# A layer with three attention branches: c_q and the gates projected as columns over 512 tokens, heads transposed in 32 bits and split after the transpose

## The chip, the cores and the metric

The kernel runs on one core of a Trainium2 chip. The metric is the device time of one execution in microseconds (us), and lower is better. The core has a matrix engine (TensorE, PE in the profile; its weight loads are PEld), a vector engine (VectorE, DVE), a scalar engine (ScalarE, ACT), GpSimd (POOL), and SyncE (SP), which issues every DMA of this kernel. Each engine works through its own queue of instructions in a fixed order and waits on semaphores.

## The reference, cut to what matters

```python
h = layer_norm(x)                                   # 2048 tokens x 1024
proj = h @ w_in                                     # 1024 x 7592
(a_q, a_k, a_v, a_gate, i_q, i_k, i_w, b_q, b_k, b_v, b_gate, c_q, c_gate, m_gate) = split(proj)
# A: an indexer (i_q, i_k, i_w) picks 256 keys per query; 8 heads of a_q attend to them
o_a = dsa_attention(rope(a_q), rope(a_k), a_v, rope(i_q), rope(i_k), i_w)
o_b = diff_attention(rope(b_q), rope(b_k), b_v, lam)      # 4 heads, two softmaxes each, causal
o_c = memory_attention(c_q, mk, mv)                       # 4 heads over 256 memory tokens
y_r = (o_r * silu(r_gate)) @ w_proj_r                     # r = a, b, c
merged = sum over r of sigmoid(m_gate[r]) * y_r
out = layer_norm(2**0.25 * h + merged @ w_out)
```

All is float32. A matrix product of two float32 numbers is made of three products (`mm3`): each operand is split into a high part that the matrix engine keeps and the rest (`split`: a copy, then a subtraction).

## The kernel before

The 2048 tokens are 16 blocks of 128 (`b`), or 8 pairs of 256 (`p`). One program does it all, in this order of writing: normalise blocks 0 to 7 and transpose them (`prologue`), project a_q and the indexer columns for them (`dense_ai(0)`), find the top 256 keys of blocks 2 to 7 (`topk_group`), project b_k, b_v, b_q (`dense_b(0)`), the same for blocks 8 to 15 with two more top-k groups, then attention B (4 heads `hd`, in heads 0 and 2 from block 0 up, in 1 and 3 from block 15 down), attention A, the projections of c_q and of all gates for the upper half of the tokens (`dense_g(1)`) and the lower half (`dense_g(0)`), then branch C with the products of B and C with their output weights, then those of A (`stage1`), `w_out` and the last layer norm (`stage2`).

The order on each engine isn't the order of writing. The program is scheduled when it is built: the builder's own model of the engines decides what stands where, takes what was written first when it is ready, and moves later work up into places where an engine would stand idle. The result is one fixed queue per engine. So the matmuls of `dense_g`, which are written after both attentions but need little, are filler: they stand between the matmuls of the top-k stage and of attention B.

`dense` projects 256 columns of `w_in` per call (a job). The normalised tokens lie transposed and split in `hP[p]`, 256 tokens each. For c_q, the C gate and the merge gates the weights are the stationary side, 128 columns, and 256 tokens stream past (columns as output rows). For the A and B gates (`sg`, `idx[0]` 0 and 1) a block of 128 tokens is stationary and 256 weight columns stream past. Either way a matmul has a stationary 128x128 tile and streams 256 columns, and a pair of tokens takes 2 x 8 x 3 = 48 of them. `emit` evicts each result (tile `do`) and stores it.

`heads_out` takes the projected and rotated heads `o` of a pair from SBUF to a transposed, split form in DRAM: for each of the two blocks it splits them on DVE (tile `dt`, lines 68 and 69), transposes high and low parts together (4 matmuls against `idr`, line 223), and ACT copies the PSUM tile to `de` (line 225). It is called 64 times.

`gated` multiplies a branch's output by its stored gate (line 830, on POOL for B, on DVE for A), transposes the product on PE (line 833), and splits it on ACT and DVE (lines 835 and 836) into `oT`, which feeds the output product `yps`.

In attention B a block's chain is: logits `lg` (lines 623, 624, PE), copy with a running minimum (633, 637, DVE), exponentials (691, ACT), sums and the difference of the two softmaxes (694 to 697, DVE), transposes `pt` (703, PE), the split `pr` (66 on ACT, 69 on DVE), products `ops` (709, PE), and the norm of the output (712 to 724, ACT, DVE, POOL). `lg` has two buffers, `pt` two, `ops` one, `P` four.

## Time and profile before

| what | value |
|---|---|
| device time, median of 3 runs (range) | 2966.72 us (2961.39 to 2970.45) |
| span of the profiled execution, first to last instruction | 2965.9 us |
| PE busy | 2830.5 us (95%) |
| PEld busy | 2715.7 us (92%) |
| DVE busy | 2279.2 us (77%) |
| ACT busy | 1442.6 us (49%) |
| POOL busy | 983.2 us (33%) |
| 16 DMA engines | 40.2% of their time in the hardware queue |

The profiled execution's span is 0.8 us below the median of the runs, so times of the trace and times of runs can be used side by side. Matmuls overlap in the array: one 256-column matmul is recorded as 284 ns long, but the next one starts much sooner. The cost of a matmul in a full queue is therefore read from how many start in a stretch and not from the length of a record. "Busy" on PE counts a stretch as busy while any matmul is in the array.

### The profile page before, as it was taken

How to read it: one execution, taken by the hardware profiler on the slowest of the kernel's cores; microseconds unless marked ns; L12 is line 12 of the kernel's file. 1: busy time of each engine (PE TensorE's matmuls, PEld its weight loads, DVE VectorE, ACT ScalarE, POOL GpSimd, SP SyncE). 2: the span in 40 equal slices, each digit the busy share in tenths (PEclk: the TensorE clock that was granted, in tenths of full speed). 3: DMA queues.
4: the chain of work that ended last, by engine and by line, in shares of the span. 5: the costliest groups of instructions: out<-in, count | busy, mean ns of one | idle time of the engine just before them, and what ended most of it. 6: DMA issues, size and time to landing. Idle time of an engine off the chain costs nothing. (4 is left out here: it accounts for less than half of the span.)

```text
span 2965.9 us, 57460 instructions
## 1 busy us (share of the span) xinstructions
PE 2830.5 (95%) x21616; PEld 2715.7 (92%) x21616; DVE 2279.2 (77%) x5309; ACT 1442.6 (49%) x2806; POOL 983.2 (33%) x1064
## 2 busy tenths in 40 slices
PE   7979998999999998999999999999999999988998
PEld 6979998999999998999999999988999999978887
DVE  6499988999899998676667766658787777776655
ACT  4345673677266772333344334446566556544100
POOL 6663547242522236323324222302222222200221
PEclk9999999999999999999999999999999999999999
DMA  6554434433232234624234242273433333256532
GB/s 208 171 191 138 159 113 156 133 119 114 94 101 76 82 93 147 201 73 140 89 118 142 77 128 80 75 242 110 133 114 119 102 113 102 86 172 224 172 131 79
DMA packets 320949, 379.47 MB, mean 128 GB/s; under 512 B 26400, under 2 KB 236832, under 8 KB 320160
## 3 DMA queue, kind: packets, MB, share of 16 engines
q1 hardware_dynamic: 320672, 375.80, 40.2%
q8 instruction: 171, 2.80, 0.4%
q14 instruction: 106, 0.87, 0.1%
HBM read 236.02 MB, written 139.69 MB: 127 GB/s over the span
## 5 line engine op out<-in xcount | busy, mean ns | idle before, releaser
L72 PE MATMUL dps<-hP,w 128*128 128x256 f32 x2048 | 582.6, 284 | 15.1 <-DVE do L69 9.9
L74 PE MATMUL dps<-hP,w 128*128 128x256 f32 x2048 | 581.7, 284 | 0.0
L73 PE MATMUL dps<-hP,w 128*128 128x256 f32 x2048 | 581.2, 284 | 0.0
L72 PE MATMUL dps<-w,hP 128*128 128x256 f32 (+1 forms) x1664 | 491.1, 296 | 12.5 <-POOL w L64 3.1
L73 PE MATMUL dps<-w,hP 128*128 128x256 f32 (+1 forms) x1664 | 490.0, 295 | 0.0
L74 PE MATMUL dps<-w,hP 128*128 128x256 f32 (+1 forms) x1664 | 487.9, 294 | 0.0
L72 PEld LDWEIGHTS dps<-hP,w 128*128 128x128 f32 x2048 | 392.6, 192 | 21.6 <-DVE do L69 10.7
L74 PEld LDWEIGHTS dps<-hP,w 128*128 128x128 f32 x2048 | 392.5, 192 | 4.4 <-POOL w L69 0.3
L73 PEld LDWEIGHTS dps<-hP,w 128*128 128x128 f32 x2048 | 392.7, 192 | 3.6
L533 ACT ACTIVATE ja<-sall,thr 128x1280 bf16<-128x1280 f32 (+4 forms) x224 | 302.2, 1349 | 122.6 <-DVE thr L529 107.1
L64 POOL TENSOR_SCALAR w<-wr 128x1024 fp32r<-128x1024 f32 x120 | 135.5, 1129 | 629.5 <-PE dps L74 404.9
L72 PEld LDWEIGHTS dps<-w,hP 128*128 128x128 f32 x1664 | 324.0, 195 | 16.8 <-issue 4.3
L69 POOL TENSOR_TENSOR w<-wr,w 128x1024 fp32r<-128x1024 f32 (+1 forms) x128 | 332.1, 2595 | 15.0 <-ACT w L66 6.9
L520 DVE TENSOR_SCALAR_CACHE_REDUCE jd<-sall,thr 128x1408 bf16<-128x1408 f32 (+6 forms) x231 | 330.9, 1433 | 5.9
L73 PEld LDWEIGHTS dps<-w,hP 128*128 128x128 f32 x1664 | 324.3, 195 | 1.8
L74 PEld LDWEIGHTS dps<-w,hP 128*128 128x128 f32 x1664 | 323.8, 195 | 2.2
L691 ACT ACTIVATE P<-P,nm 128x128 f32<-128x128 f32 (+15 forms) x128 | 154.1, 1204 | 197.8 <-DVE nm L690 187.5
L626 DVE CUSTOM_DVE_ANT_0 AP<-lg,bias 128x512 f32<-128x512 f32 (+3 forms) x304 | 181.9, 619 | 68.4 <-PE lg L624 25.1
L66 ACT CAST apr<-apt 128x512 fp32r<-128x512 f32 (+1 forms) x288 | 158.4, 563 | 141.7 <-PE apt L777 108.4
L633 DVE TENSOR_SCALAR_CACHE_REDUCE P<-lg 128x512 f32<-128x512 f32 (+3 forms) x288 | 170.4, 596 | 72.3 <-PE lg L624 71.2
L493 DVE SCALAR_TENSOR_TENSOR sall<-ir,iw,sall 128x512 f32<-128x512 f32 (+3 forms) x266 | 217.1, 865 | 8.9 <-ACT ir L489 8.0
L782 PE MATMUL aops<-apr,VA 128*128 128x256 f32 x1088 | 206.7, 297 | 16.8 <-DVE apr L69 6.7
(249 smaller groups left out, 7109.2 us busy)
## 6 DMA issues: line engine op xcount, KB each, us to landing
wr<-in_w_in_dram SPq DMA_DIRECT2D x112, 512.0 KB, 3.9
tm_d<-do SPq DMA_DIRECT2D x96, 256.0 KB, 2.1
bq<-qb_d SPq DMA_DIRECT2D x128, 128.0 KB, 3.1
aq<-qa_d SPq DMA_DIRECT2D x128, 128.0 KB, 3.1
yt<-tm_d SPq DMA_DIRECT2D x64, 256.0 KB, 3.6
sg_d<-do SPq DMA_DIRECT2D x48, 256.0 KB, 2.1
ys<-sg_d SPq DMA_DIRECT2D x48, 256.0 KB, 3.1
facc<-mg_d SPq DMA_DIRECT2D x48, 256.0 KB, 4.1
```

What stands on the lines that cost most here:

```text
L66: A.copy(H, src)
L69: el.tensor_tensor(L, src, H.bitcast(F32), op=ALU.subtract)
L72: PE.matmul(ps, lH, rH, start=start, stop=False)
L73: PE.matmul(ps, lH, rL, start=False, stop=False)
L74: PE.matmul(ps, lL, rH, start=False, stop=stop)
L493: V.scalar_tensor_tensor(s[:, c0:c0 + cn], r[:, :cn], iw[:, h:h + 1], s[:, c0:c0 + cn], op0=ALU.mult, op1=ALU.add)
L520: V.tensor_scalar(jd[:, :L], sc[b], t.bitcast(F32)[:, i:i + 1], None, op0=op, op1=ALU.add, accum_out=dst[:, i:i + 1])
L533: A.activation(ja[:, :L], sc[b], AF.Sign, bias=thr.bitcast(F32)[:, i:i + 1], scale=-1.0, accum_out=cnt[:, i:i + 1])
L626: V.tensor_tensor_reduce(P[:, c0:c0 + cn], ps[:, :cn], bias[:, c0:c0 + cn], scale=-0.125, scalar=-LOW, op0=ALU.add, op1=ALU.min, accum_out ...
L633: V.tensor_scalar(P[:, c0:c0 + n0], ps[:, :n0], -0.125, None, op0=ALU.mult, op1=ALU.min, accum_out=mx[:, col, nch:nch + 1])
L691: A.activation(p[:, :L], p[:, :L], AF.Exp, bias=nm[:, c:c + 1], scale=-1.0, accum_out=sm[:, c:c + 1])
L782: PE.matmul(o_ps.rearrange("p a d -> p (a d)"), VA[:, k0 + i], pr[:, a, i].rearrange("p e q -> p (e q)"), start=(k0 + i == 0 and a == 0), ...
```

## The change

It has three parts.

1. The transposed tokens lie in one tile `H4` with two halves of 512 tokens (a quad `q` is 4 blocks). `dense` projects c_q, all the sigmoid and silu gates (also those of A and B) with the weights stationary and 512 tokens streaming: 24 matmuls of 512 columns for 128 weight columns and a quad. `emit_gate` evicts one 128x512 tile. The stored gates and c_q are laid out per quad, and the loads take 128 or 256 of 512 tokens of each row.
2. `heads_out` no longer splits on DVE first. It transposes the heads as float32 against `idf` (4 matmuls for two blocks, with 128 columns each or fewer), into one PSUM bank, and then splits on ACT and DVE into `de` on the way out. High and low parts are stored as separate planes. The loads of `qi` become four DMAs per tile in place of one; `kg` is loaded as two planes.
3. `gated` transposes the branch's output before the gate. DVE multiplies the transposed result by the transposed gate, ACT makes the high part, POOL subtracts to make the low part. The product ahead of the transposes is gone.

```diff
-    def heads_out(o, nh, d, dup, stores, p):
-        e = dp.tile([128, nh, 2, 128], F32R, name="de")
-        for i in range(2):
-            t = dp.tile([128, nh, 2 * dup, d], F32R, name="dt" if nh > 1 else "dt1", bufs=3 if nh > 1 else 2)
...
-            split(t[:, :, 0:dup], t[:, :, dup:2 * dup], src, V, V)
...
-            for c in range(nh):
-                PE.transpose(pt[:, c], t[:, c].rearrange("p a d -> p (a d)"), idr)
-            with tc.high_priority():
-                A.copy(e[:, :, i], pt)
+    def heads_out(o, groups, stores):
+        n = len(groups)
+        e = dp.tile([128, 2, n, 2, 128], F32R, name="de", bufs=4)
+        turn[0] ^= 1
+        if turn[0]:
+            pt = dq2.tile([128, n, 2, 128], F32, name="psT")
+        else:
+            pt = dqs.tile([128, n, 2, 128], F32, name="dpt", bufs=1)
+        for u, (c0, cn) in enumerate(groups):
+            for i in range(2):
+                PE.transpose(pt[:cn, u, i], o[:, i, c0:c0 + cn], idf)
+        for u0, u1 in ((0, 2),) if groups[-1][1] == 128 else ((0, n - 1), (n - 1, n)):
+            cn = groups[u0][1]
+            with tc.high_priority():
+                split(e[:cn, 0, u0:u1], e[:cn, 1, u0:u1], pt[:cn, u0:u1], A, V)
...
+        if kind in ("cq", "sg", "tm"):
+            for q in range(2 * half, 2 * half + 2):
+                for g in range(2):
+                    c = slice(g * 128, (g + 1) * 128)
+                    ps = dqs.tile([128, 512], F32, name="dps")
+                    for k in range(KT):
+                        mm3(ps, w[:, 0, k, c], w[:, 1, k, c], H4[:, q % 2, 0, k], H4[:, q % 2, 1, k], k == 0, k == KT - 1)
+                    with tc.high_priority():
+                        emit_gate(kind, idx, g, q, ps)
+            return
...
-                SP.dma_start(qi.bitcast(F32), qi_d[j][b // 2][:, :, (b % 2) * 128:(b % 2 + 1) * 128])
+                src = qi_d[j][b // 2][:, :, (b % 2) * 128:(b % 2 + 1) * 128].rearrange("a (h d) t -> a d h t", h=4)
+                for r in range(4):
+                    SP.dma_start(qi.bitcast(F32)[32 * r:32 * r + 32], src[r // 2])
...
-        SP.dma_start(s, sg_d[r][b // 2][b % 2])
-        eng.tensor_tensor(o, o, s, op=ALU.mult)
+        SP.dma_start(s, sg_d[r][b // 4][:, :, 128 * (b % 4):128 * (b % 4) + 128])
...
-            A.activation(oT[:, 0, :, t], ps, AF.Copy, scale=0.5)
-            V.scalar_tensor_tensor(oT[:, 1, :, t], ps, 0.5, oT[:, 0, :, t].bitcast(F32), op0=ALU.mult, op1=ALU.subtract)
+            V.scalar_tensor_tensor(s, ps, 0.5, s, op0=ALU.mult, op1=ALU.mult)
+            A.copy(oT[:, 0, :, t], s)
+            G.tensor_tensor(oT[:, 1, :, t], s, oT[:, 0, :, t].bitcast(F32), op=ALU.subtract)
```

The changed program is scheduled anew, so whole queues stand in another order. Two places show it.

The first is PE at the end of attention B, head 3, around the logits of block 5 (`lg` 256 columns wide). `dps` are the filler matmuls of `dense_g`, `hP_25602` is a pair of blocks, `ops`, `pt` and `lg` belong to attention B. Before:

```order
L72 MATMUL dps<-hP_25602,w 128x256
L709 MATMUL ops<-vg,pr 128x256
L73 MATMUL dps<-hP_25602,w 128x256
L74 MATMUL dps<-hP_25602,w 128x256
L72 MATMUL dps<-hP_25602,w 128x256
L623 MATMUL lg<-kg,bq 128x256
L624 MATMUL lg<-kg,bq 128x256
L73 MATMUL dps<-hP_25602,w 128x256
```

After, the same place (`lg` is now on lines 628 and 629, `pt` on 708, `ops` on 714):

```order
L714 MATMUL ops<-vg,pr 128x256 x5
L628 MATMUL lg<-kg,bq 128x256
L629 MATMUL lg<-kg,bq 128x256
L708 MATMUL pt<-idf,P 128x128 x6
L628 MATMUL lg<-kg,bq 128x256
L629 MATMUL lg<-kg,bq 128x256
L714 MATMUL ops<-vg,pr 128x256
```

No filler stands there any more: the last `dps` row of the changed program is in block 11 of head 2, and the 20 blocks of attention B behind it stand alone on PE. Before, `dps` rows go on to the end of attention B and a little past it.

The second is DVE beside the indexer's scores (`sall`), where `heads_out` of the early projections stands. Before:

```order
L493 SCALAR_TENSOR_TENSOR sall<-ir,iw,sall 128x256
L493 SCALAR_TENSOR_TENSOR sall<-ir,iw,sall 128x512
L69 TENSOR_TENSOR dt<-do,dt 128x4x64 x2
L68 CAST dt<-do 128x4x64
L493 SCALAR_TENSOR_TENSOR sall<-ir,iw,sall 128x256
```

After:

```order
L498 SCALAR_TENSOR_TENSOR sall<-ir,iw,sall 128x512
L498 SCALAR_TENSOR_TENSOR sall<-ir,iw,sall 128x128
L70 TENSOR_TENSOR de<-psT,de 128x512
L496 TENSOR_SCALAR sall<-ir,iw 128x512
L500 MEMSET sall 64x64
```

The casts and subtractions ahead of the transposes (`dt`) are replaced by one subtraction behind them (`de`), of twice the width, for a pair.

## Rows read from the trace of the kernel before

**Rows 1.** Windows by stage: us, busy us (instructions) of each engine, PE clock, DMA.
```profile
0.00:200.00 200.00, 166.43 (x1231) 162.14 (x1231) 136.28 (x248) 83.13 (x162) 131.97 (x174) 0.96 0.59 197
200.00:915.00 715.00, 675.67 (x5454) 666.54 (x5453) 662.27 (x1233) 428.37 (x822) 313.95 (x312) 0.98 0.38 123
915.00:1194.00 279.00, 263.75 (x2163) 262.06 (x2162) 249.49 (x304) 160.47 (x191) 108.45 (x48) 0.98 0.35 109
1194.00:1940.00 746.00, 741.30 (x5783) 718.60 (x5783) 510.69 (x1731) 294.84 (x563) 232.16 (x336) 1.00 0.35 109
1940.00:1956.00 16.00, 16.00 (x135) 16.00 (x134) 1.20 (x6) 1.69 (x3) 1.16 (x4) 1.00 0.80 240
1956.00:2740.00 784.00, 749.17 (x5741) 705.92 (x5740) 590.61 (x1603) 453.48 (x1033) 145.74 (x144) 0.99 0.45 136
2740.00:2966.00 226.00, 218.20 (x1120) 184.41 (x1120) 128.69 (x188) 20.66 (x35) 49.76 (x47) 0.98 0.38 132
```

**Rows 2.** Instructions on the tiles `ips`, `pf`, `lg`: ns min/median/max, first and last start.
```profile
L484 PE MATMUL ips<-KI,qi x560: 218/281/415, 136.9 to 915.2; 128*128 128x256 f32 x172, 128*128 128x128 f32 x15
...
L571 DVE TENSOR_SCALAR pf<-ja x14: 253/510/2673, 459.7 to 1181.2; 128x384 bf16<-128x384 bf16 x1, 128x512 bf16<-128x512 bf16 x1, 128x640 bf16<-128x640 bf16 x1, 128x768 bf16<-128x768 bf16 x1
...
L623 PE MATMUL lg<-kg,bq x320: 220/390/500, 1193.8 to 1922.8; 128*128 128x512 f32 x136, 128*128 128x128 f32 x8, 128*128 128x256 f32 x8, 128*128 128x384 f32 x8
```

**Rows 3.** Windows, columns as in Rows 1: `dps` alone on PE, then `fz` alone.
```profile
1050.00:1125.00 75.00, 75.00 (x627) 75.00 (x627) 67.55 (x99) 46.22 (x53) 29.60 (x16) 1.00 0.30 92
2750.00:2830.00 80.00, 80.00 (x344) 64.38 (x343) 50.45 (x73) 6.58 (x12) 22.98 (x21) 1.00 0.44 151
```

**Rows 4.** Timeline of PE, transposes: start us, us, engine, line, names, form, count.
```profile
431.32 0.46 PE L223 MATMUL dpt<-idr,dt 128*128 128x128 f32 x4
...
1324.39 1.03 PE L703 MATMUL pt<-idf,P 128*128 128x128 f32 x8
```

**Rows 5.** Groups of DVE instructions: busy us, mean ns | idle before, releasers.
```profile
L69 DVE TENSOR_TENSOR pr<-pt,pr 128x512 fp32r<-128x512 f32 x112 | 76.3, 686 | 35.2 <-ACT pr L66 35.2
L69 DVE TENSOR_TENSOR dt<-do,dt 128x256 fp32r<-128x256 f32 x128 | 76.1, 620 | 0.2
...
L68 DVE CAST dt<-do 128x256 fp32r<-128x256 f32 x128 | 50.0, 415 | 42.8 <-POOL do L136 31.9 <-PE dpt L223 8.7 <-PE psT L223 1.4
```

**Rows 6.** Window 1685:1940, all instructions, then `lg`, `pt`, `ops` alone; PE, PEld, DVE first.
```profile
1685.00:1940.00 255.00, 253.60 (x1989) 246.36 (x1988) 164.13 (x550) 100.57 (x181) 74.39 (x108) 1.00 0.30 92
...
1685.00:1940.00 255.00, 60.81 (x210) 32.81 (x210) 67.16 (x233) 1.00 0.30 92
...
1685.00:1940.00 255.00, 28.04 (x194) 22.25 (x194) 33.91 (x56) 27.54 (x56) 1.00 0.30 92
...
1685.00:1940.00 255.00, 59.64 (x395) 52.24 (x393) 5.94 (x21) 5.55 (x21) 1.00 0.30 92
```

**Rows 7.** Waits of DVE, window 1685:1940: us in total, times, longest.
```profile
DVE P L633 <- PE lg L624: 32.5, 30, 2.4
DVE pr L69 <- ACT pr L66: 17.7, 10, 3.6
DVE o L724 <- POOL rsb L723: 14.8, 10, 4.4
DVE rc L694 <- ACT P L691: 12.3, 10, 2.2
DVE o L714 <- ACT oh L712: 11.5, 11, 3.1
```

**Rows 8.** Line 830 in `gated`, B on POOL and A on DVE: ns min/median/max.
```profile
L830 POOL TENSOR_TENSOR yo<-yo,ys x16: 1260/1290/1429, 1988.3 to 2505.9; 128x512 f32<-128x512 f32 x16
...
L830 DVE TENSOR_TENSOR fo<-fo,ys x16: 681/693/693, 2604.5 to 2875.8; 128x512 f32<-128x512 f32 x16
```

**Rows 9.** Windows around a pause of PE, columns as in Rows 1.
```profile
1154.00:1158.00 4.00, 0.49 (x5) 0.29 (x3) 4.00 (x2) 0.02 (x1) 2.13 (x1) 0.99 0.15 23
1158.00:1168.00 10.00, 5.23 (x24) 5.23 (x25) 9.78 (x10) 0.89 (x3) 7.43 (x3) 0.50 0.46 156
```

More of the change, by code (lines that the diff above doesn't have):

```diff
@@ L82, in tile_layer @@
     h_d = [dram(f"h_d{b}", [128, D]) for b in range(NB)]
-    qa_d = [[dram(f"qa_d{j}_{p}", [4, 128, 256]) for p in range(NP)] for j in range(2)]
-    qi_d = [[dram(f"qi_d{j}_{p}", [128, 4, 256]) for p in range(NP)] for j in range(2)]
+    qa_d = [[dram(f"qa_d{j}_{p}", [2, 256, 256]) for p in range(NP)] for j in range(2)]
+    qi_d = [[dram(f"qi_d{j}_{p}", [2, 128, 256]) for p in range(NP)] for j in range(2)]
     ka_d = dram("ka_d", [128, S])
@@ L250, in dense @@
             for i in range(2):
-                if kind in ("cq", "tm") or (kind == "sg" and idx[0] == 2):
-                    c = slice(i * 128, (i + 1) * 128)
-                    h = hP[p]
-                    for k in range(KT):
-                        mm3(ps[:, i], w[:, 0, k, c], w[:, 1, k, c], h[:, 0, k], h[:, 1, k], k == 0, k == KT - 1)
-                    continue
-                h = hT[2 * p + i]
+                h = hT_of(2 * p + i)
                 for k in range(KT):
@@ L295, in dense_ai01, with emit_gate @@
                 emit("ai1", None, p, None, W_AI - 256, o[1])
-    def emit(kind, idx, p, ps, n, o=None):
-        if kind == "cq":
-            for i in range(2):
-                o = dw.tile([128, 2, 256], F32R, name="do", bufs=3)
-                with tc.high_priority():
-                    split(o[:, 0], o[:, 1], ps[:, i], A, V)
-                SP.dma_start(cq_d[p][:, 2 * idx + i], o.bitcast(F32))
-            return
+    def emit_gate(kind, idx, g, q, ps):
+        if kind == "cq":
+            for a in range(2):
+                o = dw.tile([128, 512], F32R, name="do", bufs=3)
+                if a == 0:
+                    A.copy(o, ps)
+                    H = o
+                else:
+                    V.tensor_tensor(o, ps, H.bitcast(F32), op=ALU.subtract)
+                SP.dma_start(cq_d[q][:, 2 * idx + g, a], o.bitcast(F32))
+            return
+        r, j = idx
+        o = dw.tile([128, 512], F32, name="do", bufs=3)
+        A.activation(o, ps, AF.Tanh, scale=0.5)
+        if kind == "sg":
+            V.scalar_tensor_tensor(o, o, 1.0, ps, op0=ALU.add, op1=ALU.mult)
+        SP.dma_start((sg_d if kind == "sg" else tm_d)[r][q][:, 2 * j + g], o)
+    def emit(kind, idx, p, ps, n, o=None):
         if kind != "bv" and o is None:
             o = dw.tile([128, 2, 256], F32, name="do", bufs=3)
-        if kind in ("sg", "tm"):
-            r, j = idx
-            with tc.high_priority():
-                A.activation(o, ps, AF.Tanh, scale=0.5)
-                if kind == "sg":
-                    V.scalar_tensor_tensor(o, o, 1.0, ps, op0=ALU.add, op1=ALU.mult)
-            if kind == "tm" or r == 2:
-                SP.dma_start((sg_d if kind == "sg" else tm_d)[r][p][:, 2 * j:2 * j + 2], o)
-            else:
-                SP.dma_start(sg_d[r][p][:, :, j * 256:(j + 1) * 256].rearrange("i p c -> p i c"), o)
-            return
         if kind == "bv":
-            v = dp.tile([128, 2, 2, 2, 128], F32R, name="de")
+            v = dp.tile([128, 2, 2, 2, 128], F32R, name="de", bufs=4)
             with tc.high_priority():
@@ L349, in emit @@
             rope_apply(dp, vi, 5, 4, 32, p)
[L350 to L361 removed]
+            kd = ki_d.rearrange("(g a d) t -> g d a t", g=2, a=2)
+            heads_out(o, [(0, 128), (128, 32)],
+                      lambda e: [(kd[g][:, :, tok], e[0:32, :, 1].rearrange("d a i t -> d a (i t)")) for g in range(2)] +
+                                [(qi_d[1][p].rearrange("a p t -> p a t"), e[:, :, 0].rearrange("p a i t -> p a (i t)"))])
             iwt = dp.tile([128, 2, 8], F32, name="iwt")
```

107 lines of the change are left out of this document (48 added, 59 removed).

## Prediction

> **What bounds the kernel now.** I read the windows by stage first [rows 1]. PE is in use nearly everywhere, but the stages have different limits. From 200 to 1194 us DVE is busy 662 of 715 us and 249 of 279 us: the search for the top keys runs on it, and PE has filler (dense projections) to do meanwhile. From 1194 to 1940 us, attention B, PE is busy 741 of 746 us and DVE only 511: PE is the bound, because filler stands between B's own matmuls. From 1956 to 2740 us (attention A beside the products of B and C) PE is busy 749 of 784 us and no engine is full. From 2740 us on PE is the bound again.
>
> Second come the points where stages hand over [rows 2]. The last indexer matmul starts at 915.2 us, the last step of the top-k search at 1181.2 us, and the first logits of B at 1193.8 us. So B starts when the search is over, and between 915 and 1194 us it is DVE's chain, not PE, that runs out last.
>
> Third comes the price of a matmul in a full queue [rows 3]: 627 filler matmuls of 256 columns start in 75 us, 0.1196 us each; 344 of 512 columns start in 80 us, 0.2326 us each.
>
> **Part 1, 512 columns.** There are 20 jobs for each half of the tokens. Each takes 4 pairs x 48 = 192 matmuls now and 96 afterwards, so 7680 x 0.1196 = 918.5 us become 3840 x 0.2326 = 893.2 us: 25 us less of PE work. The Trainium skill (TensorE: Matmul & The Clock Gate, "Wait — 56ns, not 53.3ns?") has a matmul cost its columns at 2.4 GHz and about 2.5 ns more, by which the same part would save only some 10 us; the spacings measured here are longer and decide.
>
> **Part 2, heads.** 64 calls take 544 transposes now (8 in each of 48 calls, 10 in each of 16) and 256 afterwards. Whole rows of the timeline give 0.46/4 = 0.115 us for the one kind and 1.03/8 = 0.129 us for the other [rows 4], 63 - 33 = 30 us. If the last 0.25 us of a row is drain for which nothing waits (an estimate from the length of these rows), it is about 0.07 and 0.11 us, 38 - 28 = 10 us. I take 13 us, since these stand among other matmuls. So PE has about 38 us less to do (35 to 55). On DVE the `dt` casts and subtractions go, 50.0 + 76.1 us, and 48 subtractions of 512 columns at 0.686 us, priced by the `pr` row, and 32 narrower ones at about half of that come, 44 us: 82 us less [rows 5]. All of it lies before 700 us. SP issues 84 more loads for `qi`; they stand ahead of the scores, two tiles ahead of use, and I cost them at nothing (1 us a block, 14 us, if that cover fails).
>
> **Part 3, gates.** For B the POOL product of 1.29 us moves from ahead of the transposes to behind the split: a chain of the same length. For A a DVE product of 0.69 us becomes a POOL subtraction, taken at the 1.29 us of the nearest row, 0.6 us longer in each of 16 blocks, while DVE gets 11 us back [rows 8]. The gate tile is held longer. I take 0, with bounds of -10 and +10 us.
>
> **What the new order does.** This decides. In the order of PE I counted what stands ahead of each mark, every matmul at the spacing of its width. Ahead of B's first logits there are 1056 us of work before and 1072 after. From there to the end of B there are 735 and 704 us. But the filler lies differently: in the changed program it makes up about two thirds of B's early blocks, against a little over half before, and it is used up in block 11 of head 2. The last 20 blocks of B stand alone on PE. A filler matmul is twice as long now and can't be broken off, so each one that is taken in pushes B's own work back further; that is how I read the order.
>
> Now the sum, stage by stage.
>
> B's start. Ahead of the last indexer matmul stand 798 us before and 817 us after. Before, PE got there at 915 us, 117 us of waits and slow clock later. DVE's 82 us of relief shorten those waits, but transposes still wait for the rotation on POOL, which is most of what `dt` waited for, 31.9 of 42.8 us [rows 5]. I take 95 us (75 to 117): 912 us. The rest of the search is unchanged and took 279 us [rows 1, 2]: B starts at 1191 us (1171 to 1213).
>
> B to block 11 of head 2. 596 us of PE work; before, this piece took 491 us for 483, so 8 us of waits: 604 us, to 1795 us. PE is the bound here; DVE needs under 350 us for it.
>
> B's last 20 blocks. Before, they fill the window 1685 to 1940 us, 255 us with filler. Alone on PE they hold 210 `lg`, 194 `pt` and 395 `ops` matmuls [rows 6], 42 + 21 + 47 = 110 us at their spacings. DVE was busy 164 us there, 1 of it for filler. It also gets the 16 subtractions of the weights for B and C, which now stand at B's end: 11 us at 0.69 us. So DVE is the bound, with a floor of 174 us. To that come waits on DVE that have nothing to do with filler: for the split's copy, for POOL's norm, for the exponentials, for the output copy, 17.7 + 14.8 + 12.3 + 11.5 = 56 us [rows 7]. The wait for `lg`, 32.5 us, goes with the filler. With DVE in less of a queue behind PE some of the 56 us overlap; I take half: 202 us (174 to 231). B ends at 1997 us, 57 us later than now. That is the main term.
>
> The hand-over to A. The loads of A's keys and values wait for B's buffers. Now 16 us lie there and PE works through filler, busy 16.00 of 16.00 us [rows 1]; afterwards PE stands still as long: 2013 us.
>
> A's stage. 714 us of PE work took 784 us; 18 us of it were leftover filler. After, 704 us with the same 70 us of waits: 774 us (760 to 790), to 2787 us. The end, 226 us, is unchanged [rows 1]. Sum: 3013 us of span; the span stands 0.8 us under the median of the runs, so 3013 us.
>
> **The rivals.** *Faster:* the relief of DVE goes through to the end. The waits ahead of the last indexer matmul fall from 117 to 55 us, B starts at 1151 us, and its tail runs at DVE's floor of 174 us: 3013 - 40 - 28 = 2945 us. For it speaks that DVE is 93% busy from 200 to 915 us; against it that PE's order now puts more work ahead of that matmul, and that DVE waited 56 us on other engines in the tail. It decides for faster as soon as B ends before about 1940 us. The Trainium skill (Perfetto Trace Analysis, "Optimizing Tensor Performance") says that larger matmuls are more efficient where possible; by it alone the 38 us of PE work would come off everywhere, 2929 us, and that is this rival's far end.
>
> *Level:* B starts at 1171 us and the tail takes 174 us: 1949 us, then 16 + 774 + 226: 2965 us.
>
> *Slower still:* PE at half clock in the tail. After a pause in which PE was busy 0.49 of 4 us, the clock is 0.50 for the next 10 us [rows 9], that is 1.2 GHz in place of 2.4. In the tail PE has 110 us of work in 200. If it runs at half most of the time, 110 become 220 us and PE is the bound with half of the waits: 248 us, 3059 us. Against it: the single waits of DVE there are 2 to 4 us at the longest [rows 7].
>
> *The change doesn't do what it says:* 512 columns cost twice 256, for example because the longer rows of `H4` are read no faster. The 25 us stay on PE; about half lie where PE is the bound: 3025 us.
>
> **How the numbers follow.** The forecast, 3013 us (2980 to 3045), has 0.55; faster 0.14; level 0.09; half clock 0.17; no gain of width 0.05. The measurement can tell about 0.3% from no change, 9 us. So faster is 0.14, within 0.3% is 0.09, and slower is 0.55 + 0.17 + 0.05 = 0.77. The range from 2958 to 3065 us leaves out most of the faster case and the upper end of the half clock.
>
> **What would show it.** In the profile after: B's first logits near 1190 us; its last `ops` near 1997 us; a stretch of some 200 us before that with DVE 80 to 90% busy and PE far from full, without `dps`; spacings of 0.233 us in filler; `dt` gone. If the last `ops` comes before 1940 us, or if PE is full in the last 200 us of B, the main term is wrong. If B starts before 1160 us, the relief of DVE was worth more than I gave it.

## The result and the profile after

| what | before | after |
|---|---|---|
| device time, median (range) | 2967.02 us (2961.39 to 2970.45), 4 runs | 3006.46 us (3003.92 to 3013.21), 4 runs |
| ratio to before, 95% interval | | 1.0135 (1.0116 to 1.0153) |
| span of the profiled execution | 2965.9 us | 3002.0 us |
| PE busy | 2830.5 us | 2806.7 us |
| PE not busy (span less busy) | 135.4 us | 195.3 us |
| DVE busy | 2279.2 us | 2202.2 us |

The change makes the kernel about 39 us slower. In the two profiles PE has 24 us less to do and DVE 77 us less, but PE stands idle 60 us longer. So the question is where those 60 us lie.

The page of the changed kernel: the total of each engine, then PE's busy tenths and its clock in 40 slices of 75 us. Lines of the code are five further down than before around attention B (`lg` on 628 and 629, `pt` on 708, `ops` on 714).

```profile
PE 2806.7 (93%) x17488; PEld 2507.5 (84%) x17488; DVE 2202.2 (73%) x5053; ACT 1399.6 (47%) x2718; POOL 1005.8 (34%) x1080
PE   7979979999999998999999998869999999997998
PEclk9989999999999999999999999979999999998999
```

The three slices with 8, 8 and 6 run from 1801 to 2026 us: the end of attention B and the hand-over to A. Windows by stage (us, then busy us and instructions of PE, PEld, DVE, ACT, POOL, the PE clock, DMA), to set beside [rows 1]:

```profile
0.00:200.00 200.00, 168.18 (x1183) 163.19 (x1184) 117.99 (x184) 79.48 (x155) 128.25 (x171) 0.93 0.59 189
200.00:927.00 727.00, 682.68 (x4389) 626.56 (x4388) 629.81 (x1069) 396.05 (x758) 332.23 (x321) 0.98 0.38 122
927.00:1205.00 278.00, 258.95 (x1109) 211.00 (x1107) 246.83 (x307) 160.62 (x189) 108.49 (x48) 0.96 0.37 118
1205.00:1815.00 610.00, 601.21 (x3263) 514.91 (x3262) 346.61 (x1181) 209.03 (x401) 194.68 (x250) 1.00 0.38 115
1815.00:1972.00 157.00, 129.65 (x784) 106.03 (x782) 143.95 (x533) 83.31 (x152) 23.13 (x76) 0.95 0.23 62
1972.00:1987.00 15.00, 0.65 (x2) 0.35 (x2) 2.29 (x12) 0.27 (x1) 2.66 (x8) 0.50 0.69 199
1987.00:2778.00 791.00, 748.99 (x5657) 702.49 (x5658) 588.49 (x1592) 450.87 (x1031) 161.81 (x157) 0.98 0.43 131
2778.00:3002.00 224.00, 216.45 (x1112) 182.97 (x1112) 126.25 (x183) 19.98 (x34) 54.59 (x50) 0.98 0.38 130
```

The marks that answer to [rows 2], with the duration in ns and the first and last start, and the last filler matmul:

```profile
L489 PE MATMUL ips<-KI,qi x560: 218/281/582, 134.0 to 926.7; 128*128 128x256 f32 x172, 128*128 128x128 f32 x15
...
L576 DVE TENSOR_SCALAR pf<-ja x14: 242/510/2475, 422.1 to 1192.7; 128x384 bf16<-128x384 bf16 x1, 128x512 bf16<-128x512 bf16 x1, 128x640 bf16<-128x640 bf16 x1, 128x768 bf16<-128x768 bf16 x1
...
L628 PE MATMUL lg<-kg,bq x320: 220/393/679, 1205.0 to 1956.4; 128*128 128x512 f32 x136, 128*128 128x128 f32 x8, 128*128 128x256 f32 x8, 128*128 128x384 f32 x8
...
L75 PE MATMUL dps<-H,w x1280: 387/389/632, 621.5 to 1786.9; 128*128 128x512 f32 x183
```

The last filler stands at 1786.9 us, in head 2. From 1815 to 1972 us, the last 20 blocks of attention B, PE is busy 130 of 157 us and DVE 144. From 1972 to 1987 us, while A's first loads are under way, PE is busy 0.65 of 15 us, where before it worked 16.00 of 16.00 us [rows 1]. These two windows hold 27 + 14 = 41 us in which PE isn't busy; before, B and the hand-over together had 5. (Busy time hides a part of it: the 130 us in the last 20 blocks are spent on 110 us of matmuls at full spacing, and PE's mean granted clock is 0.973 where it was 0.985.)

### The profile page after: what moved, and what is told of

The parts are those of the page before. It is cut to its first block, busy times and chain, and to the rows that moved or that the text cites. A ratio compares the mean times of both kernels' runs of the same rounds, so it can differ in the third digit from the quotient of the medians.

```text
span 3002.0 us, 48979 instructions
## 1 busy us (share of the span) xinstructions
PE 2806.7 (93%) x17488; PEld 2507.5 (84%) x17488; DVE 2202.2 (73%) x5053; ACT 1399.6 (47%) x2718; POOL 1005.8 (34%) x1080
## 4 chain that ended last, share of the span: by engine, by line
PE 61%; DVE 18%; issue 6%; DMA 6%; POOL 4%; ACT 3%; SPq 1%; DVEq 0%; POOLq 0%; ACTq 0%
PE dps L74 9%; PE dps L75 9%; PE dps L73 9%; DVE jd L525 4%; PE ops L714 3%; PE aops L787 3%; PE lg L628 3%; PE lg L629 3%; PE apt L782 3%; PE yps L73 2%; PE yps L74 2%; PE yps L75 2%; PE fz L73 2%; PE fz L74 2%; PE fz L75 2%
## 5 line engine op out<-in xcount | busy, mean ns | idle before, releaser
L73 PE MATMUL dps<-H,w 128*128 128x512 f32 x1280 | 505.9, 395 | 23.7 <-DVE do L318 12.0
L74 PE MATMUL dps<-H,w 128*128 128x512 f32 x1280 | 505.0, 394 | 1.1 <-DVE H L70 1.1
L75 PE MATMUL dps<-H,w 128*128 128x512 f32 x1280 | 503.9, 394 | 0.2 <-POOL w L70 0.2
L73 PE MATMUL dps<-w,H 128*128 128x256 f32 (+1 forms) x1152 | 344.6, 300 | 15.8 <-POOL w L65 8.2
L74 PE MATMUL dps<-w,H 128*128 128x256 f32 (+1 forms) x1152 | 343.7, 299 | 5.3 <-POOL w L70 5.3
L75 PE MATMUL dps<-w,H 128*128 128x256 f32 (+1 forms) x1152 | 343.0, 299 | 0.0
L73 PEld LDWEIGHTS dps<-H,w 128*128 128x128 f32 x1280 | 242.7, 190 | 76.7 <-issue 12.8
L74 PEld LDWEIGHTS dps<-H,w 128*128 128x128 f32 x1280 | 242.5, 189 | 50.4 <-DVE H L70 1.9
L75 PEld LDWEIGHTS dps<-H,w 128*128 128x128 f32 x1280 | 242.8, 190 | 49.5 <-POOL w L70 0.5
L498 DVE SCALAR_TENSOR_TENSOR sall<-ir,iw,sall 128x512 f32<-128x512 f32 (+3 forms) x266 | 232.5, 930 | 52.7 <-ACT ir L494 51.3
L73 PEld LDWEIGHTS dps<-w,H 128*128 128x128 f32 x1152 | 226.6, 197 | 18.7 <-POOL w L65 8.9
L74 PEld LDWEIGHTS dps<-w,H 128*128 128x128 f32 x1152 | 226.5, 197 | 7.0 <-POOL w L70 6.4
L75 PEld LDWEIGHTS dps<-w,H 128*128 128x128 f32 x1152 | 226.3, 196 | 0.8
L73 PE MATMUL yps<-yoT,H 128*128 128x256 f32 x768 | 222.4, 291 | 0.3
L70 DVE TENSOR_TENSOR apr<-apt,apr 128x512 fp32r<-128x512 f32 (+1 forms) x288 | 186.5, 656 | 47.0 <-ACT apr L67 44.8
```

The lines of the kernel that those rows point to most:

```text
L70: el.tensor_tensor(L, src, H.bitcast(F32), op=ALU.subtract)
L73: PE.matmul(ps, lH, rH, start=start, stop=False)
L74: PE.matmul(ps, lH, rL, start=False, stop=False)
L75: PE.matmul(ps, lL, rH, start=False, stop=stop)
L498: V.scalar_tensor_tensor(s[:, c0:c0 + cn], r[:, :cn], iw[:, h:h + 1], s[:, c0:c0 + cn], op0=ALU.mult, op1=ALU.add)
```

## The experiments

They run in three groups. In the expectations, theory 1 is the one of the prediction: filler is used up too early, so PE stands idle at the end of B and at the hand-over. Rival 2 blames the new layout of the heads and its narrower loads, rival 3 the late start of B (the indexer's scores held behind filler), rival 4 the gates. Theory 5, first named for e8, is theory 1 widened: PE is full as long as each block of B has some filler. Further theories are explained where they came up. "PE work" in them is a count of all matmuls in the order of PE, each at the spacing of its width.

This table has all but e11. B's start is the start of the first `lg`; the last three columns split the time in which PE is not busy, each window less PE's busy time in it.

| kernel | median us | ratio to before (95%) | B's start | PE busy | not busy: ahead of B | B and hand-over | after |
|---|---|---|---|---|---|---|---|
| before | 2967.0 | | 1193.8 | 2830.5 | 88 | 5 | 43 |
| after | 3006.5 | 1.0135 (1.0116 to 1.0153) | 1205.0 | 2806.7 | 95 | 50 | 50 |
| e1, 256 columns | 2964.7 | 0.9994 (0.9981 to 1.0007) | 1151.8 | 2821.9 | 88 | 10 | 43 |
| e2, heads only | 2959.8 | 0.9968 (0.9953 to 0.9983) | 1142.8 | 2819.5 | 83 | 10 | 44 |
| e8, without the heads | 3034.0 | 1.0226 (1.0189 to 1.0263) | 1254.4 | 2826.9 | 100 | 48 | 50 |
| e4, wide in the upper half | 2990.3 | 1.0071 (1.0049 to 1.0093) | 1213.6 | 2803.3 | 99 | 30 | 52 |
| e7, wide in the lower half | 3021.6 | 1.0177 (1.0150 to 1.0203) | 1154.2 | 2821.6 | 92 | 47 | 53 |
| e3, held by jobs | 3024.8 | 1.0194 (1.0169 to 1.0219) | 1204.2 | 2805.0 | 99 | 57 | 54 |
| e5, paced by quarters | 2999.7 | 1.0108 (1.0082 to 1.0135) | 1207.8 | 2806.6 | 98 | 41 | 52 |
| e6, paced, upper half narrow | 2984.3 | 1.0043 (1.0024 to 1.0063) | 1159.9 | 2812.2 | 98 | 31 | 42 |
| e9, finely held | 2978.4 | 1.0032 (1.0020 to 1.0044) | 1205.7 | 2788.9 | 101 | 32 | 51 |
| e10, finely held, upper half narrow | 2987.0 | 1.0057 (1.0035 to 1.0079) | 1159.3 | 2818.3 | 95 | 24 | 54 |
| e12, finely held, later | 2987.3 | 1.0070 (1.0051 to 1.0090) | 1202.2 | 2795.1 | 113 | 28 | 48 |

(In e12 the column ahead of B ends at 1209 us.)

### Which part costs the time: e1, e2, e8

e1 undoes only the width:

```diff
-                    for k in range(KT):
-                        mm3(ps, w[:, 0, k, c], w[:, 1, k, c], H4[:, q % 2, 0, k], H4[:, q % 2, 1, k], k == 0, k == KT - 1)
+                    for i in range(2):
+                        t = slice(256 * i, 256 * i + 256)
+                        for k in range(KT):
+                            mm3(ps[:, t], w[:, 0, k, c], w[:, 1, k, c], H4[:, q % 2, 0, k, t], H4[:, q % 2, 1, k, t], k == 0, k == KT - 1)
```

> The changed kernel with one thing undone: each column job goes through its 512 tokens as two runs of 256 columns into the same PSUM tile. Layouts, heads and gates stay as changed. In the order of PE this puts filler back to the end of attention B and past it (1827 us of PE work ahead of the last dps row, the last ops row at 1753). Theory 1 (the loss is PE standing idle in B's tail and at the hand-over, because the filler is used up): PE work 2722 us, idle as in the kernel before (about 138 us ahead of B, 8 in B, none at the hand-over, 82 after): about 2940 us (2920 to 2955), so faster than before. Rival 2 (the new layout of the heads and its narrower loads cost the time): stays near 3000 us. Rival 3 (the indexer's scores are held behind filler, B starts late): here the last ips has 758 us of PE work ahead of it instead of 817, so this rival also gives some 2950 us and is told apart by the held kernel. Rival 4 (the gates moved behind the transposes cost the time): stays near 3000 us.

e2 does only the second part, on the kernel before (`heads_out` and the loads, as in the diff of the change; columns and gates as before):

```diff
-            heads_out(v, 4, 64, 1, [(dst.rearrange("c p t -> p c t"), 0, 4)], p)
+            heads_out(o, [(0, 128), (128, 128)],
+                      lambda e: [(dst.rearrange("a (u p) t -> p (a u) t", u=2), e.rearrange("p a u i t -> p (a u) (i t)"))])
```

> The kernel before with only the second part of the change: heads transposed once in 32 bits and split afterwards, with the new layouts and loads of q, k and qi. Columns stay 256 wide, gates as before. Theory 1: the part itself is a gain: 13 us of PE work and 82 us of DVE work less, filler to the end of B: about 2940 us (2920 to 2955). Rival 2 (new layout and loads cost the time): 2985 us or more. Rival 3 (scores held behind filler) and rival 4 (gates): about 2940 us.

e8 does the rest without it (the same lines the other way round, in the changed kernel):

> The changed kernel with its second part undone: heads split on DVE first and transposed in high and low parts, with the layouts and loads of the kernel before; 512 columns and gates as changed. Theory 5: PE work 2706 us, last dps at 1648 us of it with 141 us of B's own work behind it: idle 134 ahead of B, about 70 in B, 15 at the hand-over, 98 after: about 3020 us (3005 to 3035). Rival 2 (the new layouts and loads cost time): 2980 us or less.

Measured: 2964.7, 2959.8 and 3034.0 us. So the second part is no cost but a gain: 27 us in the changed kernel (3034.0 to 3006.5, e8 inside its range) and about 9 us on the kernel before (0.9968 of it). Rival 2 is out. e1 and e2, measured side by side, differ by the gates of part 3, by the A and B gates as columns, and by the evictions and layouts for 512 tokens: together 5 us net. Rival 4 can be more than that only if the others give back what it costs; no run has the gates alone. The width alone is worth 3006.5 - 2964.7 = 42 us of loss: PE busy falls by 15 us, and PE not busy grows by 54, of which 40 lie in B and the hand-over.

But theory 1 gave e1 and e2 2940 us, a gain of 27, and got 2 (not clear of the noise) and 9. Windows of e2, from B's start on (B, hand-over, A's stage, the end):

```profile
1143.00:1897.00 754.00, 744.12 (x5793) 721.51 (x5794) 526.38 (x1740) 296.25 (x567) 233.32 (x338) 1.00 0.37 111
1897.00:1914.00 17.00, 17.00 (x143) 17.00 (x142) 1.60 (x7) 1.97 (x4) 4.62 (x6) 1.00 0.81 233
1914.00:2724.00 810.00, 773.25 (x5863) 727.35 (x5863) 592.92 (x1596) 456.56 (x1035) 147.71 (x146) 0.98 0.42 131
2724.00:2957.00 233.00, 225.42 (x1202) 192.12 (x1200) 130.37 (x195) 21.93 (x36) 50.45 (x47) 0.99 0.40 138
```

B starts 51 us earlier than before (1142.8 us against 1193.8): the relief of DVE arrives there. But A's stage takes 810 us where it took 784, with PE busy 773 us where it was 749 [rows 1], B takes 754 us in place of 746, and the end 233 in place of 226. Filler that PE no longer does while it waits for the search it does later: 7388 `dps` matmuls stand ahead of B where there were 7610, and after B they go on to 1971 us as before, now 57 us into A's stage. Against the kernel before, e2 has 11 us less of busy PE and 2 us more of idle; e8 against the changed kernel has 20 us more of busy PE and 3 us more of idle, with B starting 49 us later. With PE in use nearly all the time, an earlier start of B gave nothing by itself here; only less work or less idle time on PE did.

### Which half of the filler: e4, e7

The width is a choice for each half of the tokens (`half == 1` is the upper one, whose jobs are filler beside the search; `half == 0` the lower one, in B):

```diff
-                    for k in range(KT):
+                    for t in (slice(0, 256), slice(256, 512)) if half == 0 else (slice(0, 512),):
+                        for k in range(KT):
```

(e7 has `half == 1` there.)

> The changed kernel with the jobs of the lower half of the tokens, which lie in attention B, as two runs of 256 columns; those of the upper half, which lie beside the top-k search, stay 512 wide. Theory 1: B starts as late as in the changed kernel (near 1205 us), but filler lasts to 12 us of PE work ahead of the last ops: PE work 2708 us, idle 133 ahead of B, 8 in B, 15 at the hand-over, 98 after: about 2960 us (2940 to 2975). Rival 3 (scores held behind wide filler): B starts late here too, so at least 2990 us. Rivals 2 and 4: near 3000 us.

> The changed kernel with the upper half's jobs (beside the top-k search) as two times 256 columns, the lower half's (in B) 512 wide and not paced. Theory 5: B starts near 1152 us and the last dps stands at 1695 us of PE work, with 96 us of B's own work behind it: PE work 2708 us, idle 134 ahead of B, about 40 in B, 15 at the hand-over, 98 after: about 2995 us (2980 to 3010). Rival 3 (the start of B decides): about 50 us faster than the changed kernel, 2955 us.

Both lie above their forecast, by 30 and 27 us. e4's 2990.3 us is what rival 3 said (at least 2990), so it doesn't refute it, though e4 is 16 us faster than the changed kernel with B starting 9 us later. e7 refutes it: it starts B 51 us earlier than the changed kernel, at 1154 us, and ends 15 us later, with 15 us more of busy PE and 3 us less of idle. The halves don't add up: against e1 the wide upper half alone costs 26 us, the wide lower half alone 57, both together 42. The windows of e7, B with filler, B's last blocks alone, the hand-over:

```profile
1154.00:1871.00 717.00, 703.64 (x3783) 601.60 (x3782) 404.42 (x1322) 240.08 (x450) 218.75 (x278) 0.99 0.39 117
1871.00:1985.00 114.00, 94.72 (x561) 76.81 (x559) 105.22 (x409) 62.21 (x120) 18.89 (x60) 0.93 0.16 47
1985.00:2000.00 15.00, 0.66 (x2) 0.40 (x3) 1.73 (x10) 0.27 (x1) 2.33 (x8) 0.50 0.71 201
```

PE is busy 95 of 114 us and 0.66 of 15 us: the same bare end as in the changed kernel, with 34 us in which PE isn't busy. The late start has its own reason, and it goes with the upper half: B starts at 1205 and 1214 us where that half is wide, at 1152 and 1154 where it is narrow. The indexer's matmuls stand among the filler there, and DVE waits for the scores. Waits of DVE for `ir` up to the last score: before, e1, the changed kernel (total us, times, longest).

```profile
DVE sall L493 <- ACT ir L489: 8.0, 23, 1.0
...
DVE sall L500 <- ACT ir L496: 6.1, 16, 1.0
...
DVE sall L498 <- ACT ir L494: 49.6, 24, 3.6
```

Since e4 keeps the lower half narrow and still loses 26 us against e1, the wide upper half isn't free: its jobs stand ahead of the scores, about 60 us more of PE's work is done ahead of B (1079 against 1018 us, counted in the order), and that filler is missing at B's end: its last `dps` starts at 1927.9 us, B ends at 1955, and PE isn't busy 30 us in B and the hand-over, against 10.

### Can the loss be had back by spreading the filler: e3, e5, e6

If bare stretches are the loss, wide filler that lasts to the end of B should be fast. e3 holds whole jobs back behind named products of attention B (an edge on PE's queue, no semaphore):

```diff
-            dense(kind, half, [(c0, 256)], idx)
+            hold = HOLD.get(i) if half == 0 else None
+            with tc.issue_after(OB[hold]) if hold else nullcontext():
+                dense(kind, half, [(c0, 256)], idx)
```

> The changed kernel with one thing added: 15 of the 20 jobs of the lower half of the tokens, from the sixth on, may not start on PE before the products of a named block of attention B (head 0 block 8 for the sixth, head 3 block 9 for the last). Matmuls stay 512 columns wide, nothing else changes; the order ahead of B stays the same, with 817 us of PE work ahead of the last ips. Filler now lasts to 12 us of PE work ahead of the last ops. Theory 1: PE work 2693 us, idle 133 ahead of B, about 10 in B, up to 15 at the hand-over, 98 after: about 2945 us (2925 to 2965). Rival 3 (B's late start is the loss): nothing changes ahead of B, so at least 2990 us. Rivals 2 and 4: at least 2990 us.

Measured 3024.8 us, slower than the changed kernel; taken alone, that fits every rival (at least 2990 us). Filler now stands in B up to 1955 us, and still:

```profile
1204.00:1983.00 779.00, 736.42 (x4045) 625.16 (x4043) 511.52 (x1713) 292.24 (x554) 222.09 (x326) 0.98 0.34 102
1983.00:1998.00 15.00, 0.92 (x3) 0.46 (x3) 2.15 (x12) 0.27 (x1) 2.33 (x8) 0.50 0.67 196
1998.00:2789.00 791.00, 744.83 (x5657) 699.46 (x5658) 587.82 (x1592) 451.55 (x1031) 162.49 (x157) 0.98 0.43 132
```

PE isn't busy 43 us within B (36 in the changed kernel) and 14 in the hand-over. I worked out the idle time per four blocks (start to start, less the spacing of each width): 9.7 us in blocks 4 to 7 of head 0, 10.6 in blocks 12 to 15, 8.2 at the end of head 1, 8.3 in blocks 4 to 7 of head 2, and some 11 in B's last four blocks, where the filler ends. Filler starts there in bunches: 14 to 25 matmuls in each 5 us from 1240 to 1260 us, none from 1260 to 1285, and none again from 1360 to 1375. A job goes in as soon as its gate opens, and then there is nothing until the next. So the bare stretch was cut into pieces, not filled, and the hand-over stayed bare. e5 and e6 hold quarters of a job (24 matmuls, 5.6 us) in place of jobs:

```diff
+                    hold = HOLD.get(piece[0]) if half == 0 else None
+                    piece[0] += 1 - half
-                    for k in range(KT):
+                    with tc.issue_after(OB[hold]) if hold else nullcontext():
+                        for k in range(KT):
```

> The changed kernel with the filler of the lower half paced more finely: each quarter of a job (24 matmuls of 512 columns, 5.6 us) may not start on PE before the products of a named block of attention B, about one and a third quarters a block, and a few are left for the hand-over to A. Ahead of B nothing changes. Theory 5 (PE is full as long as each block of B has some filler; every stretch without any costs about 3 us a block, and that is what cost the time in the changed kernel and, between its gates, in the held one): PE work 2693 us and idle 133 ahead of B, about 15 in B, none at the hand-over, 88 after: about 2930 us (2915 to 2950). Rival 6 (a wide filler matmul delays B's own chain wherever it stands, however it is spread): idle in B stays at 60 to 75 us, about 2985 us.

> As the paced kernel, but the upper half's jobs, beside the top-k search, run as two times 256 columns, so that the indexer's scores are not held (758 us of PE work ahead of the last ips instead of 817). Theory 5: B starts near 1152 us, but the filler not used ahead of it has to be done in B or after it: PE work 2708 us, idle 134 + 15 + 0 + 88: about 2945 us, 15 us slower than the paced kernel although B starts some 50 us earlier. Rival 3 (the late start of B is part of the loss): faster than the paced kernel, 2890 us or less. Rival 6: about 2995 us.

e5 measured 2999.7 us, nearer to rival 6 (2985) than to theory 5 (2930); e6 2984.3, between 2945 and 2995. The hand-over is covered in both (20.00 of 20.00 and 19.00 of 19.00 us busy), but PE isn't busy 41 and 31 us within B. In e5 27 of its idle us lie in the first eight blocks of head 0 and 18 where head 1 ends and head 2 begins, just where my plan gave 6 to 11 us of filler to four blocks. e1 has 14 to 21 us there.

### How much filler goes into a block: e9 to e12

That made me count filler matmuls, and the count is the finding of this case. `dps` alone, in the same 16 blocks of B in each kernel (from the end of block 7 of head 0 to the end of block 8 of head 1): before, e1, the changed kernel, and e11 with 128 columns.

```profile
1265.00:1527.00 262.00, 165.57 (x1206) 158.93 (x1207) 14.62 (x23) 15.17 (x27) 1.00 0.33 100
...
1224.00:1494.00 270.00, 169.60 (x1221) 162.12 (x1221) 17.61 (x27) 15.40 (x27) 0.99 0.31 95
...
1291.00:1640.00 349.00, 248.17 (x1075) 190.93 (x1075) 8.64 (x15) 24.76 (x44) 1.00 0.34 105
...
1487.00:1741.00 254.00, 148.37 (x1174) 149.30 (x1174) 0.00 (x0) 7.18 (x13) 0.99 0.24 69
```

1206, 1221, 1075 and 1174 filler matmuls stand among the same work of B, whatever their width: 8.8, 8.6, 9.6 and 8.7 in one run of filler between two matmuls of B, on average (a few long runs pull the averages up; the medians are 6, 6, 9 and 5). With 512 columns a run lasts 2.08 us in place of 1.06, and these blocks take 349 us in place of 262 us. So it isn't that a wide matmul can't be broken off, as I had written; a run has nine of them, and five would have done (e9, below, has that). The order looks as if a filler matmul cost the same at 256 and at 512 columns; that the builder prices them so is my reading of the counts and isn't shown. B takes in filler, counted in time, at a faster pace than it needs, and it runs out.

e9 therefore holds the filler in steps of three matmuls, each behind a logits matmul, so that four blocks of B get about 0.87 of what they had in e1:

```diff
-                    for k in range(KT):
-                        mm3(ps, w[:, 0, k, c], w[:, 1, k, c], H4[:, q % 2, 0, k], H4[:, q % 2, 1, k], k == 0, k == KT - 1)
+                    for k in range(KT):
+                        with nullcontext() if half else held():
+                            mm3(ps, w[:, 0, k, c], w[:, 1, k, c], H4[:, q % 2, 0, k], H4[:, q % 2, 1, k], k == 0, k == KT - 1)
```

(`held()` takes the next step's logits matmul from a list and returns the same edge as in e3.)

> The changed kernel with the filler of the lower half held in steps of three matmuls (one k of one job, 0.70 us): each step waits for a named logits matmul of attention B, so that each four blocks of B get about 0.87 of the filler that they had in the kernel with 256 columns. Ahead of B nothing changes; matmuls stay 512 wide. Theory 7 (the order puts about nine filler matmuls into each place where B's chain leaves PE free, whatever their width, so wide filler is used up in B twice as fast as B needs it; spread as the 256-column kernel spreads it, the loss is gone): a run of filler between B's own matmuls is about 1.1 to 1.3 us long instead of 2.1, PE work 2693 us, idle 135 ahead of B, about 25 in B, 10 at the hand-over, 98 after: about 2960 us (2945 to 2975). Rival 6 (wide filler idles PE in B however it is spread): 60 to 80 us idle in B, about 3000 us, as in the kernel paced by quarters.

e10 is the same with the upper half narrow, as in e6, and about 0.97 of e1's filler for four blocks, since more of it is left; e12 is e9 with the steps held some 20 us longer and 0.85 in place of 0.87; e11 is e1 with four runs of 128 columns.

> As the finely held kernel, with the upper half's jobs as two times 256 columns, so that the scores are not held and more filler is left for B (about 440 us instead of 390) and for the hand-over. Theory 7: PE work 2708 us, idle 135 ahead of B, about 20 in B, none or little at the hand-over, 90 after: about 2955 us (2940 to 2970), B starting near 1152 us. Rival 6: about 2995 us. Rival 3 (B's start decides): some 50 us faster than the finely held kernel.

> As the finely held kernel, with the steps held somewhat longer (about 20 us of filler that stood around B's start now stands in B's last blocks and at the hand-over). In the finely held kernel the window 1922 to 1953 us, the last blocks and the hand-over, had PE busy 9.9 of 31 us, and the rest of B 705 of 716. Theory 7 (bare stretches are what is left of the loss): those 21 us mostly go, about 2960 us (2945 to 2970), level with or slightly faster than the kernel before. Rival 9 (the filler only moves the hole: B's first blocks, or the search, are bare instead): 2973 us or more.

> The changed kernel with each column job as four runs of 128 columns: a probe of the order, not of the time. Theory 7 (the order counts filler matmuls, not their length): between B's own matmuls in the blocks from head 0 block 8 to head 1 block 8 a run of filler has 8 to 10 matmuls again, now some 0.55 us long, and much filler is left when B ends (the last dps long after the last ops). Rival 8 (a wide matmul can't be broken off, which is why its runs are long): the runs stay near 1 us, 16 or 17 matmuls, and filler ends with B as with 256 columns. Time by theory 7: at least that of the 256-column kernel, 2965 us, since 128-column matmuls cost as much or more for a column.

e9 measured 2978.4 us: 28 of the changed kernel's 39 us of loss are gone, with the same matmuls, still 512 wide. It is 3 us above theory 7's range and well under rival 6's 3000. In the two profiles, 29 us apart, 11 of the gain are less idle time on PE and 18 less busy time for the same matmuls: isolated matmuls in bare stretches cost busy time too. The filler count in the 16 blocks and the windows of B, then of its last blocks with the hand-over:

```profile
1283.00:1539.00 256.00, 154.59 (x629) 110.81 (x629) 8.33 (x13) 14.52 (x25) 1.00 0.33 98
...
1206.00:1922.00 716.00, 705.02 (x3994) 610.94 (x3994) 495.44 (x1674) 288.29 (x541) 217.12 (x314) 1.00 0.36 107
1922.00:1953.00 31.00, 9.86 (x51) 7.43 (x49) 10.57 (x49) 4.39 (x14) 6.43 (x20) 0.69 0.64 204
```

629 matmuls, 1.15 us in a run, and B's main part runs with 11 us not busy. What is left is a hole of 21 us at its end: the last filler starts at 1926.5 us, and the hand-over is bare. e12 was to fill it and mostly did (in its last four blocks PE has no idle time by spacings, and 8 of 18 us of the hand-over are not busy), but it measured 2987.3 us, rival 9: the idle time came up ahead of B instead (113 us not busy against 101) and where heads change. e10 missed too, 2987.0 us against 2955 forecast: its hand-over is nearly covered, but 21 us are not busy within B, and after it 54. In all it has 11 us less of idle than e9, and 29 us more of busy PE, of which its expectation counts 15 for the narrow upper half; the other 14 are open. In e12 two of the waits within B are for a load, at the start of heads 1 and 3:

```profile
PE lg L653 <- DMA kg<-kb_d: 4.1, 1, 4.1
...
PE lg L653 <- DMA kg<-kb_d: 4.5, 1, 4.5
```

So the loss follows where the filler stands, but I didn't find a place for it that beats narrow filler: e9 has 33 us less of busy PE than e1 and 43 us more of idle. Of that, 13 lie ahead of B, where the wide upper half holds the scores, 22 in B and the hand-over, 8 behind them. Whether another spread would close them all is open; e12 closed most of the hole and opened others. The two loads above are 9 us of e12's share.

e11, measured once, doesn't tell what I wanted of it. The count held, 8.7 matmuls in a run, but a run lasts 0.96 us, not 0.55, because a matmul of 128 columns costs 0.111 us (below), nearly that of 256. So 128 against 256 can't tell counting matmuls from counting time; only 512 against 256 does. Much filler is left when B ends (the last `dps` starts at 3677 us, the last `ops` at 2150), but the price of 128 columns is reason enough for that. Much of the rest of the 4449.9 us is the clock, told at the end.

## Why the prediction came out right

The time fell 6.5 us from the forecast, 3006.5 against 3013 us, inside the range of 2958 to 3065, and on the forecast side. The mechanism held: filler is used up in block 11 of head 2, B's last 20 blocks stand alone with DVE as their bound, and PE stands still in the hand-over. But the main term was forecast too large (B ends at 1972.2 us, 32 us later than before, not 57), several terms were off, and they cancelled; that the sum came so near is in part luck. Step by step, in the profiled execution:

- **PE work, -38 us.** PE's busy time fell by 24 us; the bare stretches count in it, where isolated matmuls and half clock make busy time longer. The spacing was better than I took: 398 filler matmuls of 512 columns start in 90 us, 0.226 us each against 0.2326 from [rows 3], so the rival that width gains nothing is out.

```profile
950.00:1040.00 90.00, 90.00 (x398) 74.34 (x397) 0.00 (x0) 9.24 (x16) 1.00 0.32 102
```

- **DVE, -82 us.** It fell by 77 us, 2279.2 to 2202.2. Right, and worth little by itself: e2 has B starting 51 us earlier and gains 9 us.
- **The terms put at nothing.** The added loads of `qi` cost nothing: no wait of PE in the changed kernel ends with one. For the gates there is only the 5 us net between e1 and e2.
- **B's start, 1191 us (1171 to 1213).** It was 1205.0: inside the bounds, 14 us late. The term that was off is the waits ahead of the last indexer matmul, which DVE's relief was to shorten from 117 to 95 us: that matmul starts at 926.7 us, 110 us behind the 817 us of work. The relief came, since the second group's counting ended at 714.0 us where it had ended at 761.2. It was eaten between there and the end of the third group's first counting step (`bit`), which came 225 us later, not 165; DVE waited 49.6 us for `ir`, nearly all of it there. I had costed PE's order there by its work ahead of the last matmul alone, not by how the scores' matmuls lie among wide filler.
- **B to block 11 of head 2, 604 us.** 610 (1205 to 1815 us). Right, and PE was the bound.
- **B's last 20 blocks, 202 us (174 to 231).** 157 us, below my floor: the term that was mis-sized most. DVE is the bound, as the forecast said: busy 144 of 157 us, though PE, with 130, is not as far from full as I wrote. But the floor was too high, and the waits were too. The weight splits for B and C did not fall into this window (11 us); DVE's own work was 144 us and not 163 (the one-element `cf`, 214 ns in place of 433, is 4.6 of these 19 us; the rest isn't accounted for row by row); and of the 56 us of waits for other engines, of which I kept half, 6 us are left. Waits of DVE, window 1815 to 1972, to set beside [rows 7], and the `cf` rows of both kernels, before first:

```profile
DVE P L638 <- PE lg L629: 5.9, 8, 1.9
DVE rc L699 <- ACT P L696: 2.7, 2, 2.1
DVE o L729 <- POOL rsb L728: 2.0, 3, 0.7
DVE o L719 <- ACT oh L717: 1.0, 2, 0.8
DVE pr L70 <- ACT pr L67: 0.4, 1, 0.4
```

```profile
L696 DVE SCALAR_TENSOR_TENSOR cf<-sm,rc,nlam 128x1 f32<-128x1 f32 x20 | 8.7, 433 | 0.4
...
L701 DVE SCALAR_TENSOR_TENSOR cf<-sm,rc,nlam 128x1 f32<-128x1 f32 x19 | 4.1, 214 | 0.1
```

 A wait measured beside a full PE wasn't a wait of the chain. My reading, not tested by a run of its own: without filler the answers of PE, ACT and POOL come sooner, DVE nearly always has something to do, and the waits vanish behind it. The floor from a window with other work in it was no floor.
- **The hand-over, 16 us.** 15 us, PE busy 0.65. Right; PE's one wait there is A's first load, and the clock is at half (0.50, which is 1.2 GHz):

```profile
PE lg L628 <- DMA aq<-qa_d: 14.4, 1, 14.4
```

- **A's stage, 774 us (760 to 790).** 791. Just outside. PE's not busy time there is 42 us, before 35 [rows 1], and 84 fewer matmuls take the same 749 us of busy time. (The 18 us of leftover filler in my sum were 12 us, 92 `dps` matmuls.) The stage now begins without filler, and its first 9 us run at half clock, the row below. In e1 and e2, where filler lies over its start (up to 1981 and 1971 us), 35 and 37 us are not busy; but in e5, which has filler there too, it is 43, so the reason for the 7 us is open.

```profile
1987.00:1996.00 9.00, 6.35 (x14) 3.63 (x14) 4.68 (x14) 4.08 (x8) 0.00 (x0) 0.50 1.08 333
```

- **The end, 226 us.** 224.

The errors are +14, +6, -45, -1, +17 and -2 us, together -11: 3013 forecast for the span, 3002.0 measured.

Of the rivals, the faster one has its first condition met in e7 (B starting at 1154 us), a kernel with 15 us more of busy PE, and e7 is slower than the changed kernel: its B ends bare all the same. The half clock in the tail is out: PEclk is 0.95 from 1815 to 1972 us. The sentence of the Trainium skill (Perfetto Trace Analysis, "Optimizing Tensor Performance") that larger matmuls are more efficient where possible agrees with the trace for the matmul itself, 0.226 against 2 x 0.1196 us, and by the prediction's estimate would have had the kernel at 2929 us; the runs show the width alone as 42 us slower (e1 against the changed kernel).

The reason I gave for the early end of the filler was half wrong. That it ends in block 11 of head 2 was read from the order and is so; that a wide matmul pushes B back because it can't be broken off is not what the counts show, which have about nine matmuls in a run at either width.

The best kernel of all is e2, the second part alone: 2959.8 us, 0.9968 (0.9953 to 0.9983) of before.

## What to carry to other kernels

Where one engine is the bound nearly everywhere, add up its work and its idle time by stage; relief of another engine that moves a start earlier was worth little here (9 us for a start 51 us earlier), because the filler it displaces is done later. When filler changes size, count how many pieces the order puts between two pieces of the main work, before and after: the same number at twice the length uses it up in the wrong place and leaves a bare tail. And waits read beside a busy engine weren't a floor for the time when it is idle: 56 us became 6.

## What the runs showed of the hardware that I had not expected

In e11 a matmul of 128 columns costs nearly as much as one of 256: 361 of them start in 40 us at clock 1.00, 0.111 us each, against 0.1196 us for 256 columns [rows 3]. Each has a weight load (360 in the row, PEld busy 40.00 of 40.00 us); whether that sets the price wasn't tested. And after a single pause of PE (6.5 us for `ir`, the row below) the clock fell to 0.50, which is 1.2 GHz, and stayed there for some 690 us, although PE was busy without a gap, 300.00 of 300.00 us, on such matmuls at 0.213 us each (1408 in 300 us). It was back at 1.00 at 1440 us, when the logits of B, of up to 512 columns, had begun. A second stretch at 0.50, the last row, has PE busy 493 of 511 us. `dps` alone, then the wait, then all of PE:

```profile
700.00:740.00 40.00, 40.00 (x361) 40.00 (x360) 2.06 (x3) 2.25 (x4) 1.00 0.22 76
...
PE ips L491 <- ACT ir L496: 6.5, 1, 6.5
...
1000.00:1300.00 300.00, 300.00 (x1408) 300.00 (x1408) 156.27 (x228) 112.90 (x120) 24.93 (x13) 0.50 0.07 24
1440.00:1460.00 20.00, 20.00 (x170) 19.57 (x169) 14.79 (x63) 7.51 (x18) 2.33 (x8) 1.00 0.25 77
...
3191.00:3702.00 511.00, 493.05 (x2306) 491.94 (x2307) 13.03 (x22) 25.29 (x46) 38.60 (x25) 0.50 0.13 44
```

With 256 and 512 columns I saw no such stretch: before, the clock is 0.50 for 10 us after a pause [rows 9], and the longest stretch at 0.50 in the other runs is some 38 us, in e3 from 1972 to 2009 us with PE busy 16 of 37.
